# Emptying GpSimd's queue, smaller gate tiles and spread-out sums in layer 1 of a two-layer trunk

## The chip, the core and the metric

The kernel runs on one core of one Trainium2 chip. Its compute engines are TensorE (PE in the profile; PEld is its weight load), VectorE (DVE), ScalarE (ACT) and GpSimd (POOL). SyncE (SP) computes nothing and issues transfers, and so does POOL; the transfers of both run on the core's 16 DMA engines. Each engine takes its own instructions strictly in the order of its queue, and an instruction that waits holds up all that stand behind it on that engine. The metric is the device time of one execution in microseconds (us), the median of several runs.

## The reference

Two layers on 256 tokens of width 2048 in float32: an even one (recurrence and dilated attention) and an odd one, then a final norm. The change lies in the odd layer, "layer 1" below:

```
def odd_layer(x, norm, w_in, w_alpha, b_alpha, head_norm, v_norm, w_s, b_s, w_out):
    z = rms_norm(x, norm) @ w_in
    q, k, v, a_lr, gc, u, vd, gd = jnp.split(z, split_points(ODD_SIZES), axis=-1)
    log_a = log_sigmoid(a_lr @ w_alpha + b_alpha) / GLA_TAU
    o = gla_chunked(heads(q, 128), heads(k, 128), heads(v, 256), heads(log_a, 128))
    yc = rms_norm(o, head_norm).reshape(bsz, seq, GLA_VW) * silu(gc)
    yd = spatial_gating(gelu(u), gelu(vd), w_s, b_s, v_norm) * silu(gd)
    return concatenate([yc, yd], axis=-1) @ w_out

def spatial_gating(u, v, w_s, b_s, v_norm):      # per chunk of 128 tokens and group of 256
    v = (v - mean(v)) * rsqrt(var(v) + EPS) * v_norm
    s = einsum('gts,bcsge->bctge', tril(w_s), v) + b_s
    return u * s
```

`gla_chunked` is a gated linear attention over chunks of 64 tokens. The output of layer 1 is added to x, and the sum is normed with `final_norm`.

## The kernel before

**Products.** Every float32 weight piece ("raw", 128 x 1024, 0.5 MB) is split into two parts: ACT rounds it to `whi` (line 125) and DVE subtracts to get `wlo` (line 73, in `sub`). The activations are split in the same way, and three matmuls hi*hi, hi*lo, lo*hi (lines 133 to 135) stand for one product. SP loads the raws in order (line 119) into a pool of ten buffers; a raw is free again once its `wlo` is written. `whi` and `wlo` have four buffers each.

**Layer 1** goes through the projection in units of 512 columns. First come v and `alr` ("the units of v", `w_va` and `w_in1` units 0 and 2, lines 728 to 739). Then `pair` (line 209) runs three times: for q and k (line 765), for vd (line 854) and for u (line 922). A pair computes two units of 512 columns with seven products of half depth in place of eight. It needs sums of halves of the activations (`sums2`, made by `make_forms`, line 689) and sums of weight pieces. The latter are made by transfers that add to what lies in the buffer: after a raw's `wlo` is written, POOL issues `nc.gpsimd.dma_start(out=raw, in_=..., accum_op=ALU.add)` (line 231), 16 in each pair. A pair's first loads are the four raws x0 and the four y0, and later the four z0 (line 224); in its first run of products it uses x0[0] to x0[3], each followed by its accumulating transfer.

**The stream.** Between the steps of a pair `weave` (line 196) puts steps of the four units of gc and gd ("the stream", two matmul banks of its own): 12 steps in the first and third pair and 4 in the second. Their results go through silu into `gates` and `sgds` (lines 749 to 761), 128 x 2 x 512 tiles of the pool `big`, which has nine buffers.

**What sets the order.** The small stages are generators: `spawn` starts one, every step of the products calls `tick`, and `yield n` asks for n ticks of rest (one tick is one 512- or 256-column step of depth 128, and two in a unit of 512 columns). From the program so written a scheduler of the framework makes a fixed order for each engine, by its own estimates of durations and by which buffers are free. So a moved statement can move others on the same engine.

**The stages around the change.** `make_forms` (lines 689 to 724) makes four sums for each of two halves of the depth. `decay` (line 640) makes `la`, its rounded part `lah` (line 660) and the running sums `bp` on PE (line 665). `gla` (line 781) starts after the first pair, with `att` and a part of `kd` set to zero by POOL. After the second pair come the gate of the attention (`gla_gate`, line 877: gate times `hn`, then times the output `osb`), the norm of vd (`normed`, line 894, with `vn`), then the mixing matmuls with `wst` into `s_ps` (line 916). The transposes of the results for the last product (`transposed`, line 871) follow in and after the third pair.

Of the kernel before, what the change touches and what calls it, by code (L numbers as in the profile page):

```python
# [12 lines left out]
AF = mybir.ActivationFunctionType  # L13
ALU = mybir.AluOpType
AX = mybir.AxisListType

P = 128
# [11 lines left out]
C_ID, C_TRI, C_UP, C_IND, C_MASK, C_ONE = 0, 128, 256, 384, 512, 640  # L29
C_ALL = 768  # L30

S_GE, S_GO, S_CW, S_CB, S_BA, S_BI, S_LAM, S_BS = 0, 16, 32, 80, 92, 104, 116, 128
S_ALL = 132

NVA = 272

# [13 lines left out]

@with_exitstack
def trunk(ctx, tc, x, xt, lead, w_in0, w_out0, w_va, w_in1, w_out1, w_gate, small, dist, cst, w_alpha, w_s,
          r_balpha, r_hnorm, r_vnorm, r_fnorm, out):
    nc = tc.nc

    def pool(name, bufs, **kw):
# [254 lines left out]
    sm = one.tile([P, S_ALL], F32, name="sm")  # L311
# [108 lines left out]
    ps = by_token(w_in0, 12, act0, during=during_3)  # L420
# [172 lines left out]
    for i, (step, p0, p1) in enumerate(ORDER):  # L593
        ps = by_channel(w_in0, 16 + 2 * i, act1)
# [45 lines left out]
    def decay(alr):  # L640
# [27 lines left out]
        for b in range(2):  # L668
# [13 lines left out]
            nc.scalar.activation(dec[:, :, 2 * b:2 * b + 2], dp[:, :, :, 0], AF.Exp)  # L682
            yield 3


    sums2 = actp.tile([P, KT, 2 * T], F32R, name="sums2", tag="act")
    forms2 = [(sums2, k0, b) for k0, b in ((0, 0), (8, 0), (8, 1), (0, 1))]

    def make_forms():
        yield 6  # L690
        for i in range(2):
            def part(k0, b, lo=0):
                return act2[:, k0 + 4 * i:k0 + 4 * i + 4, lo + b * P:lo + (b + 1) * P].bitcast(F32)
# [12 lines left out]
            minus(s, part(0, 1), part(8, 1))
            minus(r, part(0, 1, T), part(8, 1, T))
            plus(s, s, r)
            keep(1, s)
            yield 3  # L710
            minus(r, part(0, 0), s)
            plus(r, r, part(0, 0, T))
            keep(2, r)
            yield 3
            minus(s, part(8, 0), r)
            plus(s, s, part(8, 0, T))
            keep(0, s)
            yield 3
            s, r = (sp_tile([P, 4, P], n) for n in ("fs", "fr"))
            minus(s, part(0, 1), part(0, 0))  # L720
            minus(r, part(0, 1, T), part(0, 0, T))
            plus(s, s, r)
            keep(3, s)
            yield 3

    v1 = [big_tile([P, 2, 512], f"vv{c}") for c in range(2)]
    spawn(make_forms())
    ps = by_token(w_va, 0, act2, n=NVA)
# [19 lines left out]

    def keep_gate(c):
        def use(ps):  # L750
            gates[c] = big_tile([P, 2, 512], f"sgc{c}")
            for b in range(2):
                nc.scalar.activation(gates[c][:, b, :], ps[b], AF.Silu, scale=rs1[:, b:b + 1])
        return use

    def keep_gd(c):
        def use(ps):
            sgds[c] = big_tile([P, 2, 512], f"sgd{c}")
            for b in range(2):
                nc.scalar.activation(sgds[c][:, b, :], ps[b], AF.Silu, scale=rs1[:, b:b + 1])  # L760
        return use

    stream = Stream([between(22, keep_gate(0)), between(26, keep_gate(1)), between(38, keep_gd(0)),
# [1 line left out]
    ps, ps_k = weave(pair(w_in1, 6, 10, act2, forms2), stream, 12)  # L765
# [8 lines left out]
                                           op0=ALU.mult, op1=ALU.mult)  # L774
    qt, kt, kd = eb, enb, ebl

    nc.gpsimd.memset(kd[64:P, 1, :], 0.0)
    osb = []
    gla_ro = []

    def gla():
# [1 line left out]
        qtt = big_tile([P, 4, T], "qtt")  # L783
        ktt = big_tile([P, 4, T], "ktt")
        att = big_tile([P, 2, 4, P], "att")
        nc.gpsimd.memset(att, 0.0)
        for src, dst, copy in ((qt, qtt, nc.scalar.copy), (kt, ktt, nc.vector.tensor_copy)):
            for b in range(2):
                tp = psa.tile([P, 4, P], F32, name="tp", tag="a")
# [32 lines left out]
        for b in range(2):  # L822
            for hp in range(2):
# [16 lines left out]
                for i in range(2):  # L840
                    square_sum(osb[b][:, hp, i * T:(i + 1) * T], sso[:, b, 2 * hp + i:2 * hp + i + 1])
                yield 2
        gla_ro.append(rsqrt_of(sso.rearrange("p a b -> p (a b)"), 8, T, "ro"))

    spawn(gla())

    wst = mid_tile([P, 4, P], "wst")
    nc.gpsimd.dma_start(out=wst, in_=w_s)

    nc.gpsimd.affine_select(out=wst, in_=wst, pattern=[[0, 4], [1, P]], compare_op=ALU.is_ge, fill=0.0,  # L850
                            base=0, channel_multiplier=-1)
    vf = []
    mv = tiny.tile([P, 8, 2], F32, name="mv", tag="mv", bufs=1)
    for c, ps in enumerate(weave(pair(w_in1, 14, 18, act2, forms2), stream, 4)):
# [8 lines left out]
    drain()  # L863
    ro = gla_ro[0]
    rv = rsqrt_of(mv[:, :, 1], 8, 1.0, "rv")
    vn = big_tile([P, 2, 512], "vn")
    nc.gpsimd.dma_start(out=vn, in_=r_vnorm.partition_broadcast(P))
    hn = big_tile([P, 2, 512], "hn")
    nc.gpsimd.dma_start(out=hn, in_=r_hnorm.partition_broadcast(P))

    def transposed(src, k0, b):
        tp = psa.tile([P, 4, P], F32, name="tp", tag="a")
        for i in range(4):
            nc.tensor.transpose(tp[:, i, :], src[:, i * P:(i + 1) * P], ident)
        split(yt1, slice(k0, k0 + 4), b * P, P, tp)

    def gla_gate(c):
        for b in range(2):
            sg = gates[c][:, b, :]
            nc.vector.tensor_mul(sg, sg, hn[:, c, :])  # L880
            for i in range(2):
                o = osb[b][:, c, i * T:(i + 1) * T]
                at = b * 4 + 2 * c + i
                nc.vector.scalar_tensor_tensor(out=o, in0=o, scalar=ro[:, at:at + 1], in1=sg[:, i * T:(i + 1) * T],
                                               op0=ALU.mult, op1=ALU.mult)
            yield 4

    def gla_out():
        for c in range(2):
            for b in range(2):  # L890
                yield 4
                transposed(osb[b][:, c, :], 4 * c, b)

    def normed(c):
        for b in range(2):
# [8 lines left out]
    yd = []  # L904
# [27 lines left out]
    def sgu_gate(c, wait):  # L932
        sg = sgds[c]
        yield wait
        nc.vector.tensor_mul(sg, sg, yd[c])
        for b in range(2):
            yield 3
            transposed(sg[:, b, :], 8 + 4 * c, b)


    spawn(sgu_gate(0, 16))
# [85 lines left out]
def layout(a):  # L1027
# [30 lines left out]
    def cols(v):  # L1058
        return v.reshape(-1, P).T

    cw = a["ev_conv_w"][0].reshape(4, NH, P).transpose(2, 1, 0).reshape(P, 48)
    small = np.concatenate([cols(a["ev_norm"][0]), cols(a["od_norm"][0]), cw, cols(a["ev_conv_b"][0]),
                            a["ev_b_a"][0].T, a["ev_b_i"][0].T, cols(a["ev_lam"][0]), a["od_b_s"][0].T], 1)
    return {
        "x": x,
        "xt": x.T.reshape(KT, P, T).transpose(1, 0, 2),
# [3 lines left out]
        "w_alpha": a["od_w_alpha"][0],  # L1070
        "w_s": a["od_w_s"][0].transpose(2, 0, 1),
        "r_balpha": a["od_b_alpha"],
        "r_hnorm": a["od_head_norm"].reshape(1, 1024),
        "r_vnorm": a["od_v_norm"].reshape(1, 1024),
        "r_fnorm": a["final_norm"].reshape(1, 2048),
    }
# [17 lines left out]
```

## Time and profile before

| | us |
|---|---|
| median of 3 runs (lowest to highest) | 915.62 (914.86 to 918.24) |
| the profiled execution: its own time | 913.44 |
| the profiled execution: span of the trace | 911.7 |
| busy: PE, DVE, ACT, POOL | 865.7, 596.5, 527.2, 56.1 |

The span is counted from the first to the last instruction. "Busy" adds up instruction times; neighbouring instructions of one engine overlap by some hundredths of a microsecond, so that a row of 0.69 us can recur every 0.60 us. A row of the waits names who waited, for what, and for how long in total. The granted clock is 1.00 at 2.4 GHz and 0.50 at 1.2 GHz. Layer 0 ends at about 484 us of the span; its order is the same in both kernels.

### The profile page before, as it was taken

The page shows a single profiled execution, that of the slowest core. Times are in us where ns is not written, and L with a number is a line of the kernel's source. Part 1 is how long each engine was busy: PE and PEld are TensorE (multiplying, and loading weights), DVE is VectorE, ACT ScalarE, POOL GpSimd, SP SyncE. Part 2 cuts the span into 40 slices and gives each one's busy share as a digit, 9 for nine tenths or more (in the row PEclk, how much of TensorE's full clock was granted, in tenths as well). Part 3 has the DMA queues.
Part 4 walks back from the last instruction along what each step waited for, and adds up shares of the span by engine and source line. Part 5 has one row for each costly group of instructions (what it writes and reads, how often), then busy time and mean ns, then how long its engine had stood idle before and what let it go on. Part 6 is the DMA issues. An engine that isn't in the chain of part 4 may idle for free.

```text
span 911.7 us, 11935 instructions
## 1 busy us (share of the span) xinstructions
PE 865.7 (95%) x4408; PEld 726.9 (80%) x4408; DVE 596.5 (65%) x851; ACT 527.2 (58%) x764; POOL 56.1 (6%) x76
## 2 busy tenths in 40 slices
PE   9999999999999999999999899889997695999996
PEld 7888888888888888888888788677675484888886
DVE  7686456586576677665567946478657863875662
ACT  6764646756756855544446656365576363754542
POOL 1100000000000000000000002121210121000000
PEclk9999999999999999999999999989999797999998
DMA  9886555464365365655535369989989497965512
GB/s 341 340 326 208 196 179 164 127 217 163 124 223 163 116 208 184 197 190 187 177 110 198 118 205 210 282 229 262 213 197 327 83 263 208 348 209 183 196 34 92
DMA packets 52138, 182.35 MB, mean 200 GB/s; under 512 B 5856, under 2 KB 6368, under 8 KB 51824
## 3 DMA queue, kind: packets, MB, share of 16 engines
q1 hardware_dynamic: 43776, 152.13, 48.4%
q0 software_dynamic: 8160, 29.40, 16.0%
q8 instruction: 34, 0.56, 0.2%
q14 instruction: 24, 0.20, 0.1%
q10 hardware_dynamic: 144, 0.07, 0.0%
HBM read 179.47 MB, written 2.10 MB: 199 GB/s over the span
## 4 chain that ended last, share of the span: by engine, by line
PE 84%; DMA 6%; DVE 6%; ACT 2%; issue 1%; ACTq 0%; DVEq 0%
PE pc L282 19%; PE ps L134 13%; PE ps L135 12%; PE ps L133 12%; PE pc L281 9%; DMA raw<-in_w_in 6%; PE ps L237 3%; PE ps L238 3%; PE ps L239 3%; DVE wlo L73 2%; ACT whi L125 1%; PE pc L284 1%; PE sc L467 1%; PE gp L551 1%; PE gp L550 1%
## 5 line engine op out<-in xcount | busy, mean ns | idle before, releaser
L73 DVE TENSOR_TENSOR wlo<-raw,whi 128x1024 fp32r<-128x1024 f32 (+1 forms) x320 | 385.1, 1212 | 233.8 <-ACT whi L125 214.2
L125 ACT CAST whi<-raw 128x1024 fp32r<-128x1024 f32 (+1 forms) x320 | 330.5, 1041 | 277.7 <-PE ps L135 97.3
L282 PE MATMUL pc<-act,whi 128*128 128x512 f32 x768 | 269.8, 395 | 0.0
L281 PE MATMUL pc<-act,wlo 128*128 128x256 f32 x720 | 208.4, 289 | 0.0
L282 PEld LDWEIGHTS pc<-act,whi 128*128 128x128 f32 x768 | 142.6, 188 | 29.4
L133 PE MATMUL ps<-whi,act 128*128 128x512 f32 (+2 forms) x352 | 133.2, 384 | 19.5 <-ACT whi L125 19.0
L281 PEld LDWEIGHTS pc<-act,wlo 128*128 128x128 f32 x720 | 135.8, 189 | 2.5 <-DVE wlo L73 0.9
L134 PE MATMUL ps<-wlo,act 128*128 128x512 f32 (+2 forms) x352 | 133.9, 381 | 2.7 <-DVE wlo L73 2.7
L135 PE MATMUL ps<-whi,act 128*128 128x512 f32 (+2 forms) x352 | 132.9, 378 | 0.0
L133 PE MATMUL ps<-whi,yt 128*128 128x512 f32 (+1 forms) x256 | 97.3, 380 | 0.0
L135 PE MATMUL ps<-whi,yt 128*128 128x512 f32 (+1 forms) x256 | 96.3, 376 | 0.0
L134 PE MATMUL ps<-wlo,yt 128*128 128x512 f32 (+1 forms) x256 | 96.2, 376 | 0.0
L133 PEld LDWEIGHTS ps<-whi,act 128*128 128x128 f32 x352 | 67.5, 194 | 33.2 <-ACT whi L125 20.2
L134 PEld LDWEIGHTS ps<-wlo,act 128*128 128x128 f32 x352 | 68.3, 194 | 17.2 <-DVE wlo L73 5.8
L135 PEld LDWEIGHTS ps<-whi,act 128*128 128x128 f32 x352 | 67.9, 193 | 11.4
L231 POOL DMA_DIRECT2D raw<-in_w_in x48 | 41.2, 858 | 333.7 <-DVE wlo L73 270.1
L135 PEld LDWEIGHTS ps<-whi,yt 128*128 128x128 f32 x256 | 48.2, 188 | 8.9
L134 PEld LDWEIGHTS ps<-wlo,yt 128*128 128x128 f32 x256 | 48.2, 188 | 8.4
L133 PEld LDWEIGHTS ps<-whi,yt 128*128 128x128 f32 x256 | 48.2, 188 | 8.4
L237 PE MATMUL ps<-whi,sums 128*128 128x512 f32 x96 | 38.8, 404 | 0.0
L239 PE MATMUL ps<-whi,sums 128*128 128x512 f32 x96 | 37.4, 390 | 0.0
L238 PE MATMUL ps<-wlo,sums 128*128 128x512 f32 x96 | 37.4, 390 | 0.0
(273 smaller groups left out, 894.3 us busy)
## 6 DMA issues: line engine op xcount, KB each, us to landing
raw<-in_w_in SPq DMA_DIRECT2D x204, 512.0 KB, 4.8
raw<-in_w_out SPq DMA_DIRECT2D x64, 512.0 KB, 4.5
raw<-in_w_in POOLq DMA_DIRECT2D x48, 512.0 KB, 9.0
raw<-in_w_va SPq DMA_DIRECT2D x8, 272.0 KB, 2.6
xs<-in_x SPq DMA_DIRECT2D x2, 1024.0 KB, 5.8
out<-xs SPq DMA_DIRECT2D x8, 256.0 KB, 2.6
first<-in_lead SPq DMA_DIRECT2D x4, 384.0 KB, 5.6
xt<-in_xt SPq DMA_DIRECT2D x6, 256.0 KB, 7.8
```

The source lines that it names most:

```text
L73: nc.vector.tensor_tensor(out=o, in0=a, in1=hi.bitcast(F32), op=ALU.subtract)
L125: nc.scalar.copy(hi, raw)
L133: nc.tensor.matmul(ps[b], xh, wh, start=first, stop=False)
L134: nc.tensor.matmul(ps[b], xh, wl, start=False, stop=False)
L135: nc.tensor.matmul(ps[b], xl, wh, start=False, stop=last)
L231: nc.gpsimd.dma_start(out=raw, in_=part(u, i), accum_op=ALU.add)
L237: nc.tensor.matmul(ps, xh, wh, start=(first and j == 0), stop=False, skip_group_check=not first)
L238: nc.tensor.matmul(ps, xh, wl, start=False, stop=False, skip_group_check=not first)
L239: nc.tensor.matmul(ps, xl, wh, start=False, stop=(j == 7), skip_group_check=not first)
L281: nc.tensor.matmul(ps[c][:, 1, :], wl, act[:, k, 0:T], start=False, stop=False)
L282: nc.tensor.matmul(ps[c], wh, act[:, k, :], start=(k == 0), stop=(k == KT - 1))
L284: nc.tensor.matmul(ps[c][:, 1, :], wl, act[:, k, 0:T], start=False, stop=False)
```

## The change

`wst` (the mixing weights) is loaded and masked by POOL before layer 1's pairs begin, and no more between the first and the second. `vn` is loaded by SP, at the start of the first pair, and no more by POOL after the second. `hn` is not loaded at all: the head norm's gain lies in the small table `sm` as columns, and is multiplied in after the transposes (`gain`), on DVE from PSUM into a new tile `xg`, instead of into the gate. The two memsets go from POOL to DVE. The gates are tiles of 128 x 512 of the pools `mid` and `sp` instead of `big`. `make_forms` rests 7 ticks instead of 3 between its sums.

```
-S_ALL = 132
+S_GE, S_GO, S_CW, S_CB, S_BA, S_BI, S_LAM, S_BS, S_HN = 0, 16, 32, 80, 92, 104, 116, 128, 132
+S_ALL = 140
...
+    wst = mid_tile([P, 4, P], "wst")
+    nc.gpsimd.dma_start(out=wst, in_=w_s)
+    nc.gpsimd.affine_select(out=wst, in_=wst, pattern=[[0, 4], [1, P]], compare_op=ALU.is_ge, fill=0.0,
+                            base=0, channel_multiplier=-1)
     sums2 = actp.tile([P, KT, 2 * T], F32R, name="sums2", tag="act")
...
             keep(1, s)
-            yield 3
+            yield 7
...
         def use(ps):
-            gates[c] = big_tile([P, 2, 512], f"sgc{c}")
+            gates[c] = [(sp_tile if c else mid_tile)([P, 512], f"sgc{c}") for b in range(2)]
             for b in range(2):
-                nc.scalar.activation(gates[c][:, b, :], ps[b], AF.Silu, scale=rs1[:, b:b + 1])
+                nc.scalar.activation(gates[c][b], ps[b], AF.Silu, scale=rs1[:, b:b + 1])
...
-    nc.gpsimd.memset(kd[64:P, 1, :], 0.0)
+    nc.vector.memset(kd[64:P, 1, :], 0.0)
...
-        nc.gpsimd.memset(att, 0.0)
+        nc.vector.memset(att, 0.0)
...
+    vn = big_tile([P, 2, 512], "vn")
+    nc.sync.dma_start(out=vn, in_=r_vnorm.partition_broadcast(P))
     spawn(gla())
-    wst = mid_tile([P, 4, P], "wst")
-    nc.gpsimd.dma_start(out=wst, in_=w_s)
-    nc.gpsimd.affine_select(...)
...
-    vn = big_tile([P, 2, 512], "vn")
-    nc.gpsimd.dma_start(out=vn, in_=r_vnorm.partition_broadcast(P))
-    hn = big_tile([P, 2, 512], "hn")
-    nc.gpsimd.dma_start(out=hn, in_=r_hnorm.partition_broadcast(P))
-    def transposed(src, k0, b):
+    def transposed(src, k0, b, gain=None):
         tp = psa.tile([P, 4, P], F32, name="tp", tag="a")
         for i in range(4):
             nc.tensor.transpose(tp[:, i, :], src[:, i * P:(i + 1) * P], ident)
+        if gain is not None:
+            xg = sp_tile([P, 4, P], "xg")
+            nc.vector.tensor_tensor(out=xg, in0=tp, in1=gain.unsqueeze(2).broadcast_to([P, 4, P]), op=ALU.mult)
+            tp = xg
         split(yt1, slice(k0, k0 + 4), b * P, P, tp)
     def gla_gate(c):
         for b in range(2):
-            sg = gates[c][:, b, :]
-            nc.vector.tensor_mul(sg, sg, hn[:, c, :])
+            sg = gates[c][b]
...
-                transposed(osb[b][:, c, :], 4 * c, b)
+                transposed(osb[b][:, c, :], 4 * c, b, sm[:, S_HN + 4 * c:S_HN + 4 * c + 4])
...
-        nc.vector.tensor_mul(sg, sg, yd[c])
+        for b in range(2):
+            nc.vector.tensor_mul(sg[b], sg[b], yd[c][:, b, :])
```

The gates of gd (`keep_gd`) change as those of gc do, and the host puts the head norm's columns into the table.

**The order on DVE at the sums of the activations**, during the units of v. `fs`, `fr` and `sums` belong to `make_forms`, `wlo` to the product units, `alr`, `la`, `eb` to `decay`. Before:

```order
L696 TENSOR_TENSOR fs<-fs,fr 128x512
L731 TENSOR_SCALAR alr<-ps,rs_4488 128x16 x2
L73 TENSOR_TENSOR wlo<-raw,whi 128x1024
L73 TENSOR_TENSOR sums_4495<-fs,sums_4495 128x4x128
L696 TENSOR_TENSOR fs<-act_3996 128x512
L696 TENSOR_TENSOR fr<-act_3996 128x512
L73 TENSOR_TENSOR wlo<-raw,whi 128x1024
...
L73 TENSOR_TENSOR wlo<-raw,whi 128x1024
L696 TENSOR_TENSOR fr<-fr,act_3996 128x512
L696 TENSOR_TENSOR fs<-act_3996 128x512
L696 TENSOR_TENSOR fs<-act_3996,fr 128x512
L73 TENSOR_TENSOR sums_4495<-fr,sums_4495 128x4x128
```

Now, at the same place of the program:

```order
L73 TENSOR_TENSOR wlo<-raw,whi 128x1024
L73 TENSOR_TENSOR sums_4498<-fr,sums_4498 128x4x128
L701 TENSOR_TENSOR fs<-act_3996,fr 128x512
L736 TENSOR_SCALAR alr<-ps,rs_4488 128x16 x2
L701 TENSOR_TENSOR fs<-fs,act_3996 128x512
L73 TENSOR_TENSOR wlo<-raw,whi 128x1024 x2
L653 TENSOR_TENSOR la<-lp,bal 128x512
...
L655 SCALAR_TENSOR_TENSOR eb<-la 128x1024
L701 TENSOR_TENSOR fr<-act_3996 128x512
L73 TENSOR_TENSOR wlo<-raw,whi 128x1024
L701 TENSOR_TENSOR fs<-fs,fr 128x512
L73 TENSOR_TENSOR wlo<-raw,whi 128x1024
```

Three weight pieces of 1024 columns have their `wlo` ahead of `la` where before there were two, the fourth and fifth come ahead of L658 instead of behind it, and the sums of the second half of the depth follow in the last unit of v.

**The order on PE at the running sums `bp`**, in the units of v. Before:

```order
L133 MATMUL ps<-whi,act_3996 128x256 x2
L665 MATMUL bp<-lah,trir 128x512
L665 MATMUL bp_4931<-lah,trir 128x512
L134 MATMUL ps<-wlo,act_3996 128x256
L135 MATMUL ps<-whi,act_3996 128x256
```

Now:

```order
L133 MATMUL ps<-whi,act_3996 128x512
L134 MATMUL ps<-wlo,act_3996 128x512
L135 MATMUL ps<-whi,act_3996 128x512
L665 MATMUL bp<-lah,trir 128x512
L666 MATMUL bp<-lal,trir 128x512
```

Before, about 55 matmuls of 256 columns stood between `lp` (line 652) and `bp`; now it is about 108, the last third of them of 512 columns.

**The order on DVE at the head of the third pair.** The first `wlo` shown is that of a stream piece. Before, the `wlo` of x0[1] comes only next to the end of the norm of vd:

```order
L73 TENSOR_TENSOR wlo<-raw,whi 128x1024
L861 BN_AGGR mv<-bs 128x2
L860 BN_STATS bs<-vf_6164 128x6 x2
L861 BN_AGGR mv<-bs 128x2
L880 TENSOR_TENSOR sgc_5397<-sgc_5397,hn 128x512
...
L884 SCALAR_TENSOR_TENSOR osb_5857<-osb_5857,ro,sgc_6084 128x256 x2
...
L73 TENSOR_TENSOR wlo<-raw,whi 128x1024
L901 TENSOR_TENSOR vf_6164<-vf_6164,vn 128x512
L73 TENSOR_TENSOR wlo<-raw,whi 128x1024 x29
```

Now:

```order
L73 TENSOR_TENSOR wlo<-raw,whi 128x1024
L863 BN_AGGR mv<-bs 128x2
L862 BN_STATS bs<-vf_6168 128x6 x2
L863 BN_AGGR mv<-bs 128x2
L73 TENSOR_TENSOR wlo<-raw,whi 128x1024
...
L296 TENSOR_SCALAR rv<-mv 128x8
L73 TENSOR_TENSOR wlo<-raw,whi 128x1024 x2
L298 RECIPROCAL rv<-rv 128x8
L900 TENSOR_SCALAR vf_6153<-vf_6153,mv,rv 128x256 x2
```

Six `wlo` instead of one stand ahead of the norm (L899 before, L900 now), the four multiplications by `hn` are gone, and the eight of `osb` stand in the second pair. On PE the first two `s_ps` matmuls moved back by some 33 matmuls behind x0[1] to x0[3] and y0[0].

## Rows read from the trace of the kernel before

**Rows 1.** Waits of PE from 484 us: total us, times, longest.
```profile
PE ps L133 <- ACT whi L125: 19.0, 3, 8.9
PE s_ps L916 <- DVE vf L901: 5.1, 2, 4.5
PE ps L238 <- DVE wlo L73: 3.9, 2, 3.1
PE bp L665 <- ACT lah L660: 3.3, 1, 3.3
PE ps L134 <- DVE wlo L73: 2.7, 5, 0.9
PE at_ps L644 <- DVE alr L731: 1.0, 1, 1.0
```

**Rows 2.** Stretches: length, busy us (PE, PEld, DVE, ACT, POOL), clock, DMA share, GB/s.
```profile
488.00:522.00 34.00, 28.08 (x190) 24.98 (x189) 32.73 (x51) 23.14 (x32) 0.00 (x0) 0.95 0.42 140
522.00:546.00 24.00, 24.00 (x115) 20.06 (x114) 11.47 (x10) 13.32 (x19) 0.90 (x1) 1.00 0.71 215
546.00:588.00 42.00, 42.00 (x187) 34.75 (x187) 25.62 (x22) 23.96 (x25) 10.30 (x12) 1.00 0.99 235
600.00:695.00 95.00, 94.44 (x438) 72.02 (x436) 69.34 (x77) 63.31 (x84) 18.50 (x23) 1.00 0.95 249
695.00:702.00 7.00, 1.99 (x7) 1.05 (x6) 2.66 (x5) 2.33 (x3) 0.89 (x1) 1.00 1.04 377
708.00:718.00 10.00, 2.15 (x5) 1.04 (x6) 8.78 (x21) 1.78 (x3) 0.00 (x0) 0.73 0.00 0
718.00:757.00 39.00, 39.00 (x163) 32.03 (x164) 25.59 (x22) 19.84 (x20) 10.27 (x12) 0.94 0.99 235
800.00:820.00 20.00, 20.00 (x102) 16.28 (x101) 15.03 (x20) 11.16 (x16) 0.55 (x1) 1.00 0.62 202
```

**Rows 3.** Timeline of DVE in the units of v: start, us, line.
```profile
505.28 1.41 DVE L653 TENSOR_TENSOR la<-lp,bal 128x512 f32<-128x512 f32 x2
516.16 1.22 DVE L73 TENSOR_TENSOR wlo<-raw,whi 128x1024 fp32r<-128x1024 f32 x1
```

**Rows 4.** Timeline of ACT in the units of v.
```profile
515.57 1.04 ACT L660 CAST lah<-la 128x1024 fp32r<-128x1024 f32 x1
```

**Rows 5.** The chain that ended last, in order of time: start, us.
```profile
499.21 0.60 DVE sums L73
...
581.46 12.38 DMA raw<-in_w_in
...
691.22 9.90 DMA raw<-in_w_in
...
750.68 14.53 DMA raw<-in_w_in
```

**Rows 6.** Timeline of POOL; in brackets its idle time before and the releaser.
```profile
546.48 0.86 POOL L231 DMA_DIRECT2D raw<-in_w_in  x1 [6.18 <-DVE wlo L73]
...
599.47 1.27 POOL L786 MEMSET att<- 128x1024 f32 x1
...
697.60 0.89 POOL L231 DMA_DIRECT2D raw<-in_w_in  x1 [13.65 <-DVE bs L860]
718.36 0.87 POOL L231 DMA_DIRECT2D raw<-in_w_in  x1 [19.86 <-DVE vf L901]
```

**Rows 7.** Groups of DVE from 702 to 718 us: count, busy us, mean ns.
```profile
L884 DVE SCALAR_TENSOR_TENSOR osb<-osb,ro,sgc 128x256 f32<-128x256 f32 x8 | 3.6, 469 | 0.0
L899 DVE TENSOR_SCALAR vf<-vf,mv,rv 128x256 f32<-128x256 f32 x8 | 3.0, 410 | 0.0
L901 DVE TENSOR_TENSOR vf<-vf,vn 128x512 f32<-128x512 f32 x4 | 2.8, 688 | 0.0
L880 DVE TENSOR_TENSOR sgc<-sgc,hn 128x512 f32<-128x512 f32 x4 | 2.6, 680 | 0.0
```

**Rows 8.** The transfer of vn, us from issue to landing.
```profile
DMA to landing us min/median/max: 12.8/12.8/12.8
```

More of the change, by code (lines that the diff above doesn't have):

```diff
@@ L30 @@
 C_ALL = 768
-S_GE, S_GO, S_CW, S_CB, S_BA, S_BI, S_LAM, S_BS = 0, 16, 32, 80, 92, 104, 116, 128
-S_ALL = 132
+S_GE, S_GO, S_CW, S_CB, S_BA, S_BI, S_LAM, S_BS, S_HN = 0, 16, 32, 80, 92, 104, 116, 128, 132
+S_ALL = 140
 NVA = 272
@@ L52, in trunk @@
 def trunk(ctx, tc, x, xt, lead, w_in0, w_out0, w_va, w_in1, w_out1, w_gate, small, dist, cst, w_alpha, w_s,
-          r_balpha, r_hnorm, r_vnorm, r_fnorm, out):
+          r_balpha, r_vnorm, r_fnorm, out):
     nc = tc.nc
@@ L713, in make_forms @@
             keep(2, r)
-            yield 3
+            yield 7
             minus(s, part(8, 0), r)
@@ L717, in make_forms @@
             keep(0, s)
-            yield 3
+            yield 7
             s, r = (sp_tile([P, 4, P], n) for n in ("fs", "fr"))
@@ L723, in make_forms @@
             keep(3, s)
-            yield 3
+            yield 7
     v1 = [big_tile([P, 2, 512], f"vv{c}") for c in range(2)]
@@ L757, in use @@
         def use(ps):
-            sgds[c] = big_tile([P, 2, 512], f"sgd{c}")
+            sgds[c] = [(sp_tile if c else mid_tile)([P, 512], f"sgd{c}") for b in range(2)]
             for b in range(2):
-                nc.scalar.activation(sgds[c][:, b, :], ps[b], AF.Silu, scale=rs1[:, b:b + 1])
+                nc.scalar.activation(sgds[c][b], ps[b], AF.Silu, scale=rs1[:, b:b + 1])
         return use
@@ L843, in gla @@
         gla_ro.append(rsqrt_of(sso.rearrange("p a b -> p (a b)"), 8, T, "ro"))
+    vn = big_tile([P, 2, 512], "vn")
+    nc.sync.dma_start(out=vn, in_=r_vnorm.partition_broadcast(P))
     spawn(gla())
-    wst = mid_tile([P, 4, P], "wst")
-    nc.gpsimd.dma_start(out=wst, in_=w_s)
-    nc.gpsimd.affine_select(out=wst, in_=wst, pattern=[[0, 4], [1, P]], compare_op=ALU.is_ge, fill=0.0,
-                            base=0, channel_multiplier=-1)
     vf = []
@@ L934, in sgu_gate @@
         yield wait
-        nc.vector.tensor_mul(sg, sg, yd[c])
+        for b in range(2):
+            nc.vector.tensor_mul(sg[b], sg[b], yd[c][:, b, :])
         for b in range(2):
             yield 3
-            transposed(sg[:, b, :], 8 + 4 * c, b)
+            transposed(sg[b], 8 + 4 * c, b)
     spawn(sgu_gate(0, 16))
@@ L1062, in layout @@
     small = np.concatenate([cols(a["ev_norm"][0]), cols(a["od_norm"][0]), cw, cols(a["ev_conv_b"][0]),
-                            a["ev_b_a"][0].T, a["ev_b_i"][0].T, cols(a["ev_lam"][0]), a["od_b_s"][0].T], 1)
+                            a["ev_b_a"][0].T, a["ev_b_i"][0].T, cols(a["ev_lam"][0]), a["od_b_s"][0].T,
+                            cols(a["od_head_norm"][0])], 1)
     return {
@@ L1072, in layout @@
         "r_balpha": a["od_b_alpha"],
-        "r_hnorm": a["od_head_norm"].reshape(1, 1024),
         "r_vnorm": a["od_v_norm"].reshape(1, 1024),
```

## Prediction

> **What bounds the kernel now.** I read the waits of PE first, then a table of stretches, then the chain, then the timelines of the engines that PE waits for. PE is busy nearly all the time, so what counts is where it stands still or runs at the low clock. In layer 1 its long waits are for `whi` of a weight piece (19.0 us in three waits), for the norm of vd in front of `s_ps` (5.1), for `wlo` (3.9 and 2.7), and for `lah` and `alr` (3.3 and 1.0) [rows 1]. They lie in three kinds of places.
>
> Place A, the units of v, 488 to 522 us: DVE is busy 32.73 of 34 us, PE 28.08, the transfers only 0.42 [rows 2]. VectorE's queue is the limit there.
>
> Places B and D, the stream's pieces late in the first and third pair: the chain runs through one transfer that needs 12.38 us and one that needs 14.53 us [rows 5]. Before each, the DMA engines are full (0.99) while PE still keeps up (42.0 of 42 and 39.0 of 39) [rows 2]. Count from the moment when the pair's second accumulating transfer is issued, 546.48 and 718.36 [rows 6], to the landing of that late piece: 581.46 + 12.38 = 593.84 and 750.68 + 14.53 = 765.21. That is 47.4 us in the first pair and 46.9 in the third, although PE's waits before it were quite different. So the end of B and of D is set by the transfers, and the transfers start to count at the second accumulation.
>
> Place C, the head of the third pair, 695 to 718 us: first a stream piece needs 9.90 us [rows 5] while the DMA engines move 377 GB/s at a share of 1.04; then, from 708 to 718, the transfers stand at 0.00 and DVE is busy 8.78 of 10 [rows 2]. POOL's second accumulation waits 19.86 us in front of 718.36, last for L901 [rows 6]: what it needs is the `wlo` of x0[1], which stands behind the norm on DVE. SP's loads wait for the same `wlo`, since that frees buffers. A DVE queue in the wrong order idles the DMA engines for ten microseconds, and D comes later by as much.
>
> **Part by part.**
>
> *Sums in the units of v (A).* 28 instructions of `make_forms` at a step of 0.60 us [rows 5] are 16.8 us of DVE. All of them lie in A now; afterwards half go to the last unit. In 522 to 546 DVE does 11.47 of 24 us [rows 2]; with 8.4 more it is 19.9, which fits on average. `bp` moves behind about 53 more matmuls. In the trace `la` starts at 505.28 and `lah` ends at 515.57 + 1.04 = 516.6 [rows 3, 4], 11.3 us; 72 matmuls of 256 columns at 0.12 and 36 of 512 at 0.23 us (estimates from 42.0 us of PE for 187 rows, 0.225 each [rows 2]) give 16.9 us between. So the wait for `lah` goes, if `wlo` is ready too: the trace has a `wlo` only from 516.16 on [rows 3], just as late, and it is the new DVE order that brings this one ahead of L658. Gain: 3.3 + 1.0 [rows 1], and the low clock: 0.95 over 34 us means a tenth of the time at 1.2 GHz, half of which is lost, 1.7 us [rows 2]. Sum 6.0 us. High end: also the whole 2.7 of L134 [rows 1], 8.7 us. Low end: `lah` or its neighbour `wlo` is late anyway, 6.0 - 3.3 = 2.7 us. I take 6.0. What is late next: `wlo` of the last unit of v.
>
> *vn and hn (C, first half).* 2 x 0.52 MB leave the stretch in which the stream piece of 691.22 waits. At 377 GB/s [rows 2] they took 2.8 us; the piece lands at 698.3 instead of 701.1. `vn` comes back at the start of the first pair on SP's queue, ahead of the stream pieces. In 522 to 546 the share is 0.71 [rows 2], 7 us of free transfer time; 0.52 MB at 235 GB/s are 2.2 us. I take 0, hidden there; if it is pushed into the full stretch behind, 2.2 us; at worst the 12.8 us that it took in the full queues [rows 8], if SP's later loads had to wait for it.
>
> The row 546 to 588 has 235 GB/s at a share of 0.99 [rows 2], with transfers of both SP and POOL in it. The Trainium skill, "DMA: Bandwidth & Descriptors", section "Issuing engines are not separate DMA queues", says that DMAs of scalar, sync and gpsimd end up on the same 16 DMA engines, and that several issuers save only issue time. By that rule moving `vn` from POOL to SP buys no bandwidth, and what it gains is only that it now travels at another time: the sum would be the one here, where a queue of its own for each issuer would make its 2.2 us vanish. The trace agrees so far as 377 GB/s at 1.04 were shared by both queues.
>
> *The order on DVE at C.* The multiplications by `hn` (2.6 us) go, those of `osb` (3.6 us) move into the second pair [rows 7], where DVE does 69.34 of 95 us [rows 2]; hidden there. What matters is that the `wlo` of x0[1] now follows that of the stream piece behind only three small statistics instructions. The piece lands at 698.3, `whi` and `wlo` follow, and the second accumulation is issued at 701.5 to 705 instead of 718.36. I take 703.5: 14.9 us earlier. Bounds: 16.9 us; and 7 us, if ACT or a buffer holds x0[1] back by half of the old wait.
>
> PE cannot simply use this: it now waits for the norm behind more matmuls. Norm 3.0 + 2.8 [rows 7], about 1 us of it overlapped, plus seven `wlo` at 1.14 and some 3 us of statistics after 699.8 put the next needed `wlo` near 715, against PE's readiness at 711; some 4 us of standing still remain. But then PE has 35 matmuls more behind it than at 717.8 before, 7.9 us, and reaches the late piece of D near 747, ahead of the transfers' 703.5 + 46.9 = 750.4. So D ends with the transfers, 765.2 - 750.4 = 14.8 us earlier (14.9 in the sum), and its wait shrinks.
>
> *Memsets and wst.* On POOL `att` cost 1.27 us [rows 6], while it waited for nobody's sake; on DVE it stands among the `wlo` of 522 to 546, with 4 us to spare after the sums. Between 0 and 1.3; I take 0. `wst` leaves a place without a wait of PE: 0.
>
> *Gain after the transposes.* Four multiplications of 0.68 us (as L880 [rows 7]) come into 800 to 820, where DVE does 15.03 of 20 and PE 20.00 [rows 2]: 17.8 of 20. Hidden; 2.7 us if not. Gate tiles in smaller pools: no row has a wait for one; 0.
>
> Sum from the profiled execution's own time: 913.4 - 6.0 - 14.9 = 892.5 us. The median of the runs lies 2.2 us above it (915.62): 894.7, rounded to **895 us**.
>
> **Rivals.**
>
> 1. *Given back to the transfers.* The pairs' transfers are the true bound also before the second accumulation, and starting them earlier only makes the head of the third pair slower: accumulations share the engines with stream pieces just when PE needs these. Only A counts: 915.6 - 6.0 = 909.6. For it: 0.99 in both pairs. Against: 0.00 for ten microseconds, which is real free time [rows 2].
>
> 2. *A comes back.* The sums fill the last unit of v in blocks of three (1.8 us) in front of a `wlo`, and PE stands there as long as before. Only C counts: 915.6 - 14.9 = 900.7. For it: 19.9 of 24 us, with in-order blocks. Against: four `wlo` buffers.
>
> 3. *Slower: stream pieces starve.* In the third pair, accumulations now run beside the stream's loads from the start. Mixed traffic made a piece take 14.53 us instead of 9.90 [rows 5], 4.6 us more. If that happens to six of the ten pieces left, and PE has no lead to hide it, 27.6 us are lost: 894.7 + 27.6 = 922. It decides from five pieces on (23 us). Against: the first pair has the same mix from 546 to 588, and PE did not wait there [rows 2].
>
> 4. *The change doesn't do what it says.* Something else holds x0[1] (a `whi` buffer, ACT's table load), POOL's second accumulation stays near 715, and A's wait is only renamed: 914 to 916.
>
> **How the numbers follow.** Forecast 0.62; rival 1 0.13; rival 2 0.13; rival 3 0.05; rival 4 0.07. The forecast's own range is 890 to 901 (A at 2.7 to 8.7, C at 12 to 16.9, `vn` up to 2.2). With rivals 1 and 2 it holds 0.88; I say 888 to 910. A measurement of this kernel can tell about 0.5% (4.6 us) from no change. Rivals 1 and 2 are faster by more than that, but a weaker form of 1 is not, so 0.02 of it goes to no change: faster 0.86, same 0.09, slower 0.05.
>
> **What would show it.** A: no wait of PE for `lah`, DVE below 0.9 from 488 to 522, no low clock there. C: POOL's second accumulation of the third pair at about 697 in the new span (718.4 - 14.9 - 6.0), no stretch of ten microseconds without transfers, no L880. From it to the landing of the late piece again 47 us. `vn` landed before 546, and the first pair's 47.4 us unchanged. Wrong would be: 47 us grown to 55 or more (rival 1), waits for `wlo` between 515 and 540 (rival 2), many waits of 3 us or more for `whi` in the third pair (rival 3).

## The result, and the profile after

| | before | after |
|---|---|---|
| median, same chip (lowest to highest), us | 915.57 (914.86 to 918.24) | 892.00 (890.41 to 893.53) |
| ratio after / before, 95% interval | | 0.9737 (0.9711 to 0.9763) |
| the profiled execution: own time / span, us | 913.44 / 911.7 | 892.16 / 890.4 |

The kernel became 2.6% faster, and 892.0 us stand against 895 predicted. PE's waits from 484 us on, with the columns of [rows 1]:

```profile
PE ps L133 <- ACT whi L125: 17.2, 3, 8.4
PE ps L134 <- DVE wlo L73: 2.4, 4, 1.2
PE ps L237 <- ACT whi L125: 0.9, 2, 0.7
PE ps L238 <- DVE wlo L73: 0.8, 1, 0.8
```

The waits for `lah`, `alr` and in front of `s_ps` are gone. The wait for `whi`, the largest, has lost only 1.8 us: PE still stands at B and at D. The stretches after, with the columns of [rows 2]:

```profile
488.00:522.00 34.00, 34.00 (x229) 30.72 (x228) 32.68 (x47) 27.48 (x37) 0.00 (x0) 1.00 0.59 190
478.00:537.69 59.69, 59.69 (x360) 52.65 (x359) 48.94 (x69) 40.32 (x59) 0.93 (x2) 1.00 0.65 201
537.00:580.00 43.00, 42.76 (x189) 35.10 (x187) 26.73 (x23) 24.12 (x25) 10.28 (x12) 1.00 1.03 252
...
690.00:697.00 7.00, 5.35 (x21) 3.73 (x22) 4.85 (x14) 4.29 (x5) 1.58 (x2) 1.00 0.83 217
697.00:707.00 10.00, 9.04 (x41) 7.18 (x39) 9.96 (x19) 7.69 (x9) 2.71 (x4) 1.00 0.95 189
...
579.00:587.00 8.00, 0.76 (x4) 0.30 (x2) 0.00 (x0) 0.99 (x2) 0.00 (x0) 0.75 0.78 242
587.00:598.00 11.00, 10.43 (x34) 8.05 (x35) 7.56 (x7) 8.49 (x10) 2.59 (x3) 0.72 0.69 146
735.00:745.00 10.00, 1.76 (x8) 1.13 (x6) 0.00 (x0) 0.91 (x1) 0.00 (x0) 0.75 0.88 276
745.00:756.00 11.00, 10.35 (x35) 8.08 (x36) 7.97 (x7) 8.58 (x10) 3.43 (x5) 0.76 0.67 155
```

From 488 to 522 us (place A) DVE is as busy as before (32.68 and 32.73 of 34 us [rows 2]), but PE does 229 matmuls there in place of 190 and doesn't stand. The head of the third pair (690 to 707) has no long stretch without transfers any more, where before there were ten microseconds at 0.00 [rows 2]. The last four rows are B and D. In the first row of each PE mostly stands, in the second it works again; the granted clock is on average 0.75 and 0.72 at B, 0.75 and 0.76 at D. For comparison, the kernel before from the same point to its own second accumulation:

```profile
478.00:546.48 68.48, 62.56 (x359) 54.19 (x359) 49.13 (x68) 40.67 (x58) 0.90 (x1) 0.98 0.55 176
```

For nearly the same matmuls (359, 360) PE needed 68.5 us before and needs 59.7 after. POOL's timeline, as in [rows 6]:

```profile
537.69 0.86 POOL L231 DMA_DIRECT2D raw<-in_w_in  x1 [5.88 <-DMA raw<-in_w_in]
541.22 0.85 POOL L231 DMA_DIRECT2D raw<-in_w_in  x1 [2.67 <-DMA vn<-in_r_vnorm]
...
690.23 0.86 POOL L231 DMA_DIRECT2D raw<-in_w_in  x1 [16.76 <-DVE bs L862]
696.27 0.87 POOL L231 DMA_DIRECT2D raw<-in_w_in  x1 [5.18 <-DVE bs L862]
```

The second accumulation of the first pair is at 537.69 (546.48 before), that of the third at 696.27 (718.36), after a wait of 5.18 us in place of 19.86 [rows 6]. The 2.67 us that name `vn` are no cost of it: e1_spread below has no `vn` there, and 2.65 us in the same place. What the accumulation of the third pair waited for is seen on DVE: the `wlo` of x0[1], between the statistics of vd.

```profile
694.60 0.16 DVE L863 BATCH_NORM_AGGREGATE mv<-bs 128x2 f32<-128x6 f32 x1
694.68 1.19 DVE L73 TENSOR_TENSOR wlo<-raw,whi 128x1024 fp32r<-128x1024 f32 x1
695.79 0.17 DVE L863 BATCH_NORM_AGGREGATE mv<-bs 128x2 f32<-128x6 f32 x1
```

The late pieces of B and D on the chain (first and last line), and between them the stream piece at the head of the third pair, as in [rows 5]:

```profile
572.62 13.29 DMA raw<-in_w_in
...
684.85 6.70 DMA raw<-in_w_in
...
729.62 14.37 DMA raw<-in_w_in
```

The late pieces land at 585.91 and 743.99. With the two second accumulations and these two landings the span falls into five pieces. The table has them for the two kernels and five of the experiments below, all with the same stream; "acc 1" and "acc 3" are the second accumulations of the first and third pair:

| us | to acc 1 | acc 1 to B's piece | to acc 3 | acc 3 to D's piece | to the end |
|---|---|---|---|---|---|
| before | 546.5 | 47.4 | 124.5 | 46.9 | 146.5 |
| after | 537.7 | 48.2 | 110.4 | 47.7 | 146.4 |
| e1_spread | 538.1 | 47.1 | 126.9 | 46.7 | 147.2 |
| e3_gain | 548.1 | 47.3 | 111.1 | 47.3 | 147.8 |
| e16_both | 538.2 | 47.3 | 111.1 | 47.6 | 147.2 |
| e6_loads | 537.6 | 48.3 | 112.4 | 48.8 | 147.3 |
| e9_vnearly | 537.8 | 47.6 | 110.8 | 47.7 | 146.1 |

So the 21.3 us between the spans are -8.8 in front of acc 1 (place A), -14.1 between B and acc 3 (place C), +0.8 in each of the two pairs, and nothing behind. Of the 14.1, the stream piece at the head of the third pair gives 1.6: it lands at 691.55, 105.6 us behind B's piece, where before it was 107.3 (691.22 + 9.90 [rows 5]). The other 12.5 lie between its landing and acc 3, 17.2 us before and 4.7 now. The queues from 537 to 580 us (packets, MB, share of 16 engines) price a transfer; these are estimates:

```profile
q0 software_dynamic: 1597, 5.81, 69.3%
q1 hardware_dynamic: 1369, 4.99, 33.5%
```

q0 is POOL's, the accumulating ones: 69.3% of 43 us are 29.8 us for 11.1 pieces of 0.524 MB, 2.7 us each. SP's plain ones on q1 take 14.4 us for 9.5 pieces, 1.5 us each.

### The profile page after: what moved, and what is told of

Read it like the earlier page. It is cut to its first block, busy times and chain, and to the rows that moved or that the text cites. A ratio compares the mean times of both kernels' runs of the same rounds, so it can differ in the third digit from the quotient of the medians.

```text
span 890.4 us, 11922 instructions
## 1 busy us (share of the span) xinstructions
PE 859.1 (96%) x4408; PEld 723.2 (81%) x4408; DVE 596.5 (67%) x855; ACT 526.7 (59%) x764; POOL 53.1 (6%) x72
## 3 DMA queue, kind: packets, MB, share of 16 engines
q1 hardware_dynamic: 43920, 152.65, 49.7%
## 4 chain that ended last, share of the span: by engine, by line
PE 87%; DMA 5%; DVE 4%; issue 2%; ACT 1%; ACTq 0%; DVEq 0%
PE pc L282 20%; PE ps L134 14%; PE ps L135 14%; PE ps L133 14%; PE pc L281 10%; DMA raw<-in_w_in 4%; PE ps L237 3%; PE ps L239 3%; PE ps L238 3%; DVE wlo L73 2%; ACT whi L125 1%; PE pc L284 1%; PE sc L467 1%; PE gp L551 1%; PE gp L550 1%
## 5 line engine op out<-in xcount | busy, mean ns | idle before, releaser
L133 PE MATMUL ps<-whi,act 128*128 128x512 f32 (+2 forms) x352 | 133.5, 382 | 17.7 <-ACT whi L125 17.2
L135 PEld LDWEIGHTS ps<-whi,yt 128*128 128x128 f32 x256 | 48.2, 188 | 8.9
L134 PEld LDWEIGHTS ps<-wlo,yt 128*128 128x128 f32 x256 | 48.2, 188 | 8.5
L133 PEld LDWEIGHTS ps<-whi,yt 128*128 128x128 f32 x256 | 48.2, 188 | 8.3
```

Of the source, the lines that this page charges most:

```text
L133: nc.tensor.matmul(ps[b], xh, wh, start=first, stop=False)
L134: nc.tensor.matmul(ps[b], xh, wl, start=False, stop=False)
L135: nc.tensor.matmul(ps[b], xl, wh, start=False, stop=last)
```

## The experiments

Each ratio is to the kernel before, run beside the experiment on the same chip. It took 917.0 to 917.9 us there, so small differences to the kernel after are better read from the ratios (0.9737 for the kernel after) than from the times.

**e1_spread: A alone.**

```
 make_forms, four times:
-            yield 3
+            yield 7
```

> The kernel before, with one edit: make_forms rests 7 ticks instead of 3 between its sums. Theory (place A belongs to the spread sums alone): the second accumulation of the first pair comes 8.8 us earlier, as in the kernel after (546.48 to 537.69), the waits of PE for lah, alr and the low clock of A go, place C stays as it was (POOL's second accumulation of the third pair still waits some 19 us). Time 915.6 - 8.8 = 907, between 905 and 909. Rival (the memsets on DVE, the early wst or the small gate tiles give part of A): 2 to 5 us only, 910 to 914.

Measured: 906.19 us, ratio 0.988 (0.9861 to 0.990). POOL in its profile:

```profile
538.11 0.86 POOL L231 DMA_DIRECT2D raw<-in_w_in  x1 [5.89 <-DMA raw<-in_w_in]
...
712.12 0.87 POOL L231 DMA_DIRECT2D raw<-in_w_in  x1 [21.12 <-DVE vf L901]
```

Acc 1 is 8.4 of the 8.8 us earlier, and acc 3 still waits 21 us for the norm. A is the spread sums; C doesn't come from there.

**e3_gain: hn and the gain alone.**

```
-    hn = big_tile([P, 2, 512], "hn")
-    nc.gpsimd.dma_start(out=hn, in_=r_hnorm.partition_broadcast(P))
...
-            nc.vector.tensor_mul(sg, sg, hn[:, c, :])
... in transposed:
+        if gain is not None:
+            xg = sp_tile([P, 4, P], "xg")
+            nc.vector.tensor_tensor(out=xg, in0=tp, in1=gain.unsqueeze(2).broadcast_to([P, 4, P]), op=ALU.mult)
+            tp = xg
```

> The kernel before, with one edit: hn is not loaded, and the gain is multiplied in after the transposes. In the order of DVE this alone puts the wlo of x0[1] behind three small statistics instructions, as in the kernel after; vn is still loaded by POOL after the second pair. Theory (C is the order on DVE): the distance from the landing of B's late piece to the second accumulation of the third pair falls from 124.5 us to about 111.8 (110.4 as in the kernel after, and 1.4 for vn's half of the 2.8 us); A stays. Time 915.6 - 14.2 + 1.4 = 903, between 901 and 905. Rival (C is the two loads in front of the pair): half of the transfers are still there, so that half of the 14.2 comes, 908 to 910, and the distance is about 117.

Measured: 902.54 us, ratio 0.984 (0.9819 to 0.9861).

```profile
682.46 0.86 POOL L867 DMA_DIRECT2D vn<-in_r_vnorm  x1
699.28 0.88 POOL L231 DMA_DIRECT2D raw<-in_w_in  x1 [15.96 <-DVE bs L860]
706.50 0.85 POOL L231 DMA_DIRECT2D raw<-in_w_in  x1 [6.34 <-DVE bs L860]
```

From B to acc 3 it takes 111.1 us, of 124.5 before, though `vn` is still issued by POOL right there. The order on DVE that the missing `hn` brings is C. The four multiplications by `hn` (2.6 us [rows 7]) went with it; no run has the order without that, so up to 2.6 of the 13.4 us may be theirs.

**e6_loads: the two loads put back.**

```
+    for i in range(2):                # behind the second pair
+        idle = big_tile([P, 2, 512], f"idle{i}")
+        nc.gpsimd.dma_start(out=idle, in_=r_vnorm.partition_broadcast(P))
```

> The kernel after, with two loads of 0.5 MB into tiles that nobody reads, issued by POOL after the second pair where vn and hn were loaded before. Theory (order on DVE): they cost what their transfers take, 2.8 us at 377 GB/s, and D moves by as much: 892.0 + 2.8 = 895, between 893 and 898. Rival (the loads made most of C's 14.2 us): 900 to 906, and POOL's second accumulation of the third pair some 8 to 14 us later. Second rival: POOL must wait for a free tile before it issues them, and the accumulations behind it starve: over 906.

Measured: 895.97 us, ratio 0.9766 (0.9746 to 0.9787).

```profile
675.63 0.55 POOL L870 DMA_DIRECT2D idle<-in_r_vnorm  x1 [2.19 <-PE ps L239]
690.28 0.89 POOL L231 DMA_DIRECT2D raw<-in_w_in  x1 [14.09 <-DVE bs L862]
698.36 0.87 POOL L231 DMA_DIRECT2D raw<-in_w_in  x1 [7.18 <-DVE bs L862]
```

Acc 3 comes 2.0 us later after B than without them, D's transfers take 1.1 more, the span 4.1 in all. The 1 MB costs 2 to 4 us where the order is the new one (0.0029 of 917.9, 2.7 us, by the ratios); it didn't make C's wait.

**e16_both: A and C, and nothing else.** The edits of e1_spread and e3_gain together.

> The kernel before with the two edits that gave most so far: 7 ticks of rest in make_forms, and no hn (gain after the transposes). The memsets stay on POOL, wst and vn where they were, the gates in big tiles. Theory (A and C add up, the other parts give next to nothing): in its profile the first pair's second accumulation at 538, from the landing of B's late piece to the third pair's second accumulation 111, both pairs' transfers 47; the time is that of the kernel after, 892, plus at most 2 for vn in C: 892 to 895. Rival (the queue of POOL, the memsets and the small gates carry some of the gain): 897 or more.

Measured: 893.44 us, ratio 0.9748 (0.9725 to 0.9771); the interval of the whole change overlaps with it. The memsets, `wst`, the small gate tiles and `vn`'s place give together nothing that these runs can tell from zero.

**e9_vnearly: vn ahead of the units of v.**

```
+    vn = big_tile([P, 2, 512], "vn")   # moved: in front of v1
+    nc.sync.dma_start(out=vn, in_=r_vnorm.partition_broadcast(P))
```

> The kernel after, with the load of vn issued by SP ahead of the units of v in place of the first pair. Theory (vn's transfer lies in the full stretch of the first pair: 48.2 us there against 47.4 before): the 48.2 fall to 47.4, D comes 0.8 us earlier, 891. Rival (vn was hidden, the 0.8 is scatter): no change, 892. Rival (the load holds up the units of v, whose pieces wait behind it): 893 to 895.

Measured: 891.86 us, ratio 0.9719 (0.9698 to 0.9739). B's piece lands at 572.69 + 12.63 = 585.32, 47.6 us behind acc 1 (537.75). The profile shows 0.6 us of the 0.8, the times show nothing: not settled by these runs, and too small to matter.

**e11_half: half of each accumulation.** This kernel leaves out half of every sum of weight pieces, so its result is not the reference's.

```
-                    nc.gpsimd.dma_start(out=raw, in_=part(u, i), accum_op=ALU.add)
+                    nc.gpsimd.dma_start(out=raw[:, 0:512], in_=part(u, i)[:, 0:512], accum_op=ALU.add)
```

> The kernel after, but every accumulating transfer adds only the first 512 of the 1024 columns, so that the weight sums are not those of the reference. Everything else, each wait and each instruction, stays. Theory (the transfers of the first and third pair set the ends of B and D): from 537 to 580 us the accumulating transfers take 69.3% of 43 us for 5.81 MB, 2.7 us for each 0.52 MB. Half of 16 of them is 21.5 us less in each pair, against waits of PE of 7.34 and 8.43 us. Both waits go, and with them the low clock behind them (10.2 us each, half of it lost): 892.0 - 15.8 - 10.2 = 866, between 864 and 872; the distance of 47 us from the second accumulation to the late piece is no longer there. Rival (B and D are a matter of order, of when buffers come free): the waits stay above 5 us each, and the time above 882.

Measured: 871.45 us, ratio 0.9502 (0.9481 to 0.9523). PE's waits from 478 us on:

```profile
PE ps L134 <- DVE wlo L73: 2.3, 3, 1.1
PE ps L238 <- DVE wlo L73: 1.7, 1, 1.7
PE ps L133 <- ACT whi L125: 0.7, 1, 0.7
```

The late piece lands 39.9 us behind acc 1 (577.75, 537.81). B and D are gone, so they are set by the amount of transfers. The expectation was some 5 us too low, because it took the whole 10.2 us of low clock as work. In the rows of B above, the low clock begins while PE still stands: behind the wait 11 us at 0.72 are 6.2 us at 1.2 GHz, half of which, 3.1, is lost. At D it is 2.6 (11 us at 0.76). 892.0 - 15.8 - 5.7 = 870.5, against 871.45 measured.

**e13_w16: more of the stream in the first pair.** If B ends with the transfers, what helps is more work for PE in front of it.

```
-    ps, ps_k = weave(pair(w_in1, 6, 10, act2, forms2), stream, 12)
+    ps, ps_k = weave(pair(w_in1, 6, 10, act2, forms2), stream, 16)
...
-    for c, ps in enumerate(weave(pair(w_in1, 14, 18, act2, forms2), stream, 4)):
+    for c, ps in enumerate(weave(pair(w_in1, 14, 18, act2, forms2), stream, 0)):
```

> The kernel after, with another share of the stream: 16 of its steps in the first pair, none in the second, 12 in the third (12, 4, 12 in the kernel after). A stream piece costs 12 matmuls of 0.225 us, 2.7 us of PE, and one plain transfer, from the row of the queues 1.5 us; a pair's 16 accumulating transfers cost 2.7 us each. Theory (B is set by the transfers): each piece more in front of B takes 1.2 us off PE's wait; about three of the four lie there, so that the 7.3 us fall to about 4 and the low clock behind them shortens: 892 - 3.5 - 2.5 = 886, 884 to 889. Rival (the four steps cover the small stages of the attention in the second pair): PE waits there instead, 890 to 900.

Measured: 883.78 us, ratio 0.9634 (0.9613 to 0.9656).

```profile
PE ps L133 <- ACT whi L125: 9.0, 3, 6.8
PE ps L134 <- DVE wlo L73: 2.2, 4, 0.8
PE ps L238 <- DVE wlo L73: 1.3, 2, 0.9
```

Of the two long waits only D's is left, and the second pair has no new one. B went wholly, not by half: three more stream pieces (8 us of PE) came in front of the late one, while it landed 49 us behind acc 1 (586.8, 537.6). By the prices above that fits: three plain pieces more (4.5 us) and one accumulation fewer in front of it (12 in place of 13, 2.7 us) make 1.8 us more than the 48.2 of the kernel after; it was 1.0. The gain is smaller than B's 7.3 us of wait and 3.1 of low clock together with 1.6 at D, because a new low stretch stands at the head of the third pair: from 681 to 692 us the granted clock is 0.69, where the kernel after has 1.00.

**e15_w14: two pieces more in the first and third pair.**

```
-    ... weave(pair(w_in1, 6, 10, act2, forms2), stream, 12)      # second pair 4, third 12
+    ... weave(pair(w_in1, 6, 10, act2, forms2), stream, 14)      # second pair 2, third 14
```

> The kernel after, with 14 steps of the stream in the first pair, 2 in the second, 14 in the third and 2 behind it (12, 4, 12 and 4 in the kernel after). Theory: two pieces more in each of the pairs whose transfers are full, of which about 1.4 in front of the wait, take 1.7 us off B and off D each, and a part of the low clock: 892 - 3.4 - 1.5 = 887, 885 to 890. Rival (the pieces behind the third pair cover its last stages, the norm of the gates and the transposes): PE waits for the transposes near the end of the layer, 890 to 896.

Measured: 895.94 us, ratio 0.9767 (0.9745 to 0.9788): slower than the kernel after (0.9737, 0.9711 to 0.9763; the two intervals just overlap) and clearly than e9_vnearly beside it (0.9698 to 0.9739). The time lies in the rival's range, but not by its reason: PE's wait for the transposes (`yt`) is only 0.5 us. Waits at B and D, and ACT's timeline at B:

```profile
PE ps L133 <- ACT sgd L765: 10.0, 1, 10.0
PE ps L133 <- ACT sgc L758: 8.1, 1, 8.1
```

```profile
589.05 1.04 ACT L125 CAST whi<-raw 128x1024 fp32r<-128x1024 f32 x1 [10.70 <-DMA raw<-in_w_in]
590.11 1.28 ACT L758 ACT_TABLE_LOAD   x1
591.40 1.27 ACT L758 ACTIVATE sgc<-ps,rs 128x512 f32<-128x512 f32 x2
```

The late piece is the stream piece loaded right behind the four z0. With 12 steps it is the eighth, the last of its unit; with 14 it is the ninth, the first of the next unit. PE needs the matmul banks of the old unit for it, and the silu that frees them stands on ACT behind the `whi` of this ninth piece, which waits 10.7 us for its transfer, and behind a table load. So PE stands from 584.05 to 592.14: 6.0 us until that `whi` is done (7.3 in the kernel after), and 2.1 more for the table load and the first silu. The piece landed 49.7 us behind acc 1 (588.94, 539.26): one plain piece more in front of it, and 1.5 us more than 48.2, just the price of one.

**h_z0: the loads of z0 one by one.**

```
-        load(z0, ua + 2)
-        yield from run(m56, f6, x0, False, ua + 2)
+        for i, step in enumerate(run(m56, f6, x0, False, ua + 2)):
+            nc.sync.dma_start(out=z0[i], in_=part(ua + 2, i))
+            yield
```

> The kernel after, with the four loads of z0 in a pair issued one by one behind the four steps that follow, and no more as one block. What it tests: the stream piece for which PE waits at B is issued by SP 1.9 us behind the four z0 (565.33 to 570.71, then 572.62) and takes 13.3 us. Theory (B and D are that piece, queued behind the block of z0 among the accumulating transfers): with at most one or two z0 ahead of it the piece lands some 3 to 5 us earlier; B and D shrink from 7.3 and 8.4 us to 3 to 5 each: 883 to 888. Rival (all of the transfers up to there must be through, in whatever order): z0 itself is late then, the waits keep their sum, 890 to 894. Rival (slower): z0 is needed right behind the four steps and lands late in all three pairs, 895 to 905.

Measured: 883.95 us, ratio 0.9638 (0.9618 to 0.9657). The time is that of the theory, but not by its reason. The chain:

```profile
574.07 12.77 DMA raw<-in_w_in
...
725.97 13.86 DMA raw<-in_w_in
```

B's piece lands at 586.84, 47.7 us behind acc 1 (539.13): no earlier. But another stream piece has slipped between the loads of z0, so PE reaches the late one at 586.85, 47.7 us behind acc 1, where in the kernel after it was there 42.1 us behind it (579.76). The late piece is the ninth here too, and what is left is the wait for its `whi`, the table load and the silu (3.2 us at each place).

**i_f21: the third pair's stream in its first 21 steps.** Shares 16, 0, 12.

```
-            while done * 28 < taken * count:
+            while done * over < min(taken, over) * count:     # over = 28, third pair: 21
```

> The kernel after, with 16 steps of the stream in the first pair and none in the second (as in the run that measured 883.8), and in the third pair still 12 steps, but spread over the first 21 steps of the pair in place of all 28: the same spacing as 16 over 28, under which B was gone. Theory (the late piece lands at its time, 47 to 49 us behind the second accumulation, and what counts is how many stream pieces PE still has to work on in front of it): D's 6.8 us go like B's, with the low clock behind them: 883.8 - 6.8 - 4 = 873, 872 to 878. Rival (the last 7 steps of the pair, now without a stream piece between them, wait for their transfers): the wait only moves behind D, 880 to 886. Rival (slower): two buffers are not enough for the stream, and PE waits for each piece, over 886.

Measured: 877.0 us, ratio 0.9557 (0.9537 to 0.9576). No wait of PE over 2.6 us is left in the pairs: D went like B.

**k_ff21: the same spacing in both pairs.** Shares 12, 4, 12; `over` is 21 in the first and third pair.

> The kernel after with its shares of the stream (12, 4, 12 and 4 behind), but in the first and the third pair the 12 steps lie within the first 21 steps of the pair. Theory (what counts is the spacing, that is the pieces that PE has in front of the late one, and not how many the pair holds in all): B and D both go, with the low clock behind them, as with the other shares: 873 to 879. Rival (B needs the four further pieces): a wait of 3 us or more stays in the first pair, 880 to 885.

Measured: 876.55 us, ratio 0.9562 (0.9538 to 0.9586). B and D are gone with the old shares too, so it is the spacing that counts. A new wait of 4.4 us stands at 609, where the second pair begins.

```profile
PE ps L133 <- ACT whi L125: 4.4, 1, 4.4
```

**j_z0_f21: i_f21 with the loads of z0 one by one.**

> The run with 16, 0 and 12 steps, the 12 over 21 (877.0 measured), with the loads of z0 issued one by one as well. Theory (both edits buy the same wait, and PE now stands still for less than 8 us in the whole of layer 1's pairs): nothing more to gain, 875 to 879. Rival (z0 as a block still delays the pieces behind it): 870 to 874. Rival (slower: z0 comes late where PE no longer waits for anything else): 880 or more.

Measured: 872.47 us, ratio 0.9518 (0.9499 to 0.9537), the fastest with the whole of the computation, 20 us below the kernel after. The first rival was right. PE's waits from 478 us on:

```profile
PE ps L133 <- ACT whi L125: 2.6, 2, 2.1
PE ps L238 <- DVE wlo L73: 1.3, 2, 0.9
PE ps L134 <- DVE wlo L73: 1.0, 2, 0.8
```

These are 4.9 us, against 7.2 in i_f21, which is 2.3 of the 4.5 us between the two. The low clock at the head of the third pair is shorter, too (i_f21, then j_z0_f21, columns of [rows 2]):

```profile
685.00:696.00 11.00, 10.96 (x35) 8.34 (x36) 10.16 (x22) 7.45 (x9) 2.59 (x3) 0.72 0.73 161
682.00:693.00 11.00, 10.50 (x39) 8.10 (x40) 10.78 (x24) 8.52 (x11) 2.58 (x3) 0.84 0.75 162
```

0.72 and 0.84 over 11 us are 6.2 and 3.5 us at 1.2 GHz, half of which is lost: 1.3 us less. The last 0.9 us stays open.

## Why the prediction was right, point by point

- *A was mis-sized*: predicted 6.0, measured 8.8, just above the high end of 8.7. PE stood for 5.9 us before (68.48 - 62.56), not 4.3: the 1.5 us that it waited for `wlo` in this place belonged to the sum and not only to its high end. And PE's busy time fell by 2.9, of which the low clock explains the 1.7 that were counted. Of the other 1.2, about 0.6 is an estimate from the way busy time is counted: at each of the four stops the last matmul stands in the trace with 0.28 us, where the step to the next is 0.12. For the rest no run has an answer. e1_spread shows that the spread sums alone do it. Rival 2 (the sums make PE wait in the last unit of v) didn't come. One sign failed: DVE did not fall below 0.9 from 488 to 522. With 32.68 of 34 us its queue is as full as before, and PE no longer waits for it. So a full queue alone was not the limit; what made PE stand was the order in it, blocks of sums in front of the `wlo`, `alr` and `la` that PE was waiting for.
- *C was right in size and cause*: 14.9 predicted, 14.1 measured, acc 3 at 696.27 where "about 697" stood. e3_gain has the cause alone (with the multiplications by `hn`), and the two loads were the small part: 1.6 us on the chain and 2.0 in e6_loads, against 2.8 predicted. That "about 697" was met so closely is partly luck: A came 2.8 us earlier than forecast, C and the first pair's transfers 1.6 later together.
- *The transfers' 47 us held*: 48.2 and 47.7. So D's piece came earlier by nearly all that acc 3 did (21.2 of 22.1 us), and rivals 1 and 3 fell. The four kernels of the table without `vn` around the first pair have 47.1 to 47.4 there, the two that load it at the pair's start 48.2 and 48.3. So `vn` cost up to 0.8 and not the 0 that was taken, within the bound of 2.2; e9_vnearly (47.6, and no shorter time) leaves that unsettled, and no run explains the 0.8 of the third pair, where no `vn` is loaded. The Trainium skill, "DMA: Bandwidth & Descriptors", section "Issuing engines are not separate DMA queues", says that DMAs of scalar, sync and gpsimd all run on the same 16 DMA engines. The 48.2 and 48.3 with `vn` on SP's queue fit that, as far as 0.8 us can show it.
- *Wrong: some 4 us of standing in C, and a shorter wait at D.* PE stood 1.2 us for the `wlo` behind the norm, and 2.9 us in the shorter waits before it. It reached D's piece 40.5 us behind acc 3 (736.75), not 43.5, and so stood there for 8.4 us, where 3.4 were forecast and 8.9 stood before. This didn't move the time, since D ends with the transfers.
- *The parts put at nothing were worth nothing*: e16_both without them is within its interval of the whole change, and no wait of PE names `xg`, a memset or a gate tile.

The sum for the profiled execution was 892.5, against 892.16. That it fits to 0.3 us is luck: A was 2.8 us too small, and against that stand 0.8 in C and 0.8 in each pair that were too good. The 3 us between 895 and 892.0 come from the step to the median: it lay 2.2 us above the profiled execution before, and 0.2 below it after.

## What to carry to other kernels

Look for the moment from which a saturated transfer phase starts to count (here the second accumulating transfer), and ask of an edit whether it moves that moment: both gains came from there, and both through the order in DVE's queue. Where such a phase ends at a fixed distance, the wait behind it can still be filled, by giving TensorE more of its work in front of the late piece: the spacing of the stream and of the z0 loads was worth another 20 us. Watch then what stands behind the late piece on an in-order engine: in e15_w14 a silu behind a waiting rounding cost more than the added work brought.

## What the runs showed of the hardware

An accumulating transfer held the DMA engines 1.8 times as long as a plain one of the same size (2.7 and 1.5 us for 0.524 MB, from the two queue rows). With half of the columns it took 1.6 us, from the same view of e11_half, again 43 us long:

```profile
q0 software_dynamic: 1726, 3.14, 43.4%
```

That is 18.7 us for 12 pieces of 0.262 MB. And the granted clock was already down while PE still stood at B and D. By the rows above, 4.0 of 10.2 us at 1.2 GHz lie in front of PE's restart at B (0.75 over 8 us, then 0.72 over 11), and 5.0 of 10.3 at D (0.75 over 10, then 0.76 over 11). That part fell on idle time and cost nothing.
